# One 512-column operand in the feed-forward up products, and operands laid at one byte modulo 512

## The chip, the cores and the metric

The kernel runs on one core of one Trainium2 chip. The metric is the device time of one execution in microseconds (us). Each version is timed in several runs, and one further execution is recorded by the profiler; all rows of the profile come from that one.

## The reference

Three transformer-like blocks run one after the other on one sequence of 256 tokens with 1024 channels, in float32. Block 1 is two kinds of attention with a merge, and a product-key expert layer (PEER). Block 2 has two layers, each with a feed-forward, a mixer (a convolution module, then a gated recurrence called HGRN) and a second feed-forward. Block 3 has two layers of sliding-window attention with a short convolution and an MLP, with 16 extra "meta" tokens. The part that the change touches most is the feed-forward of Block 2, which is computed four times:

```python
def swiglu_ffn(x, w_in, w_out):
    gate, up = jnp.split(x @ w_in, 2, axis=-1)
    return (jax.nn.silu(gate) * up) @ w_out
```

Here w_in is 1024 by 5632 and w_out is 2816 by 1024, so the hidden width is 2816 = 22 x 128. All matrices are read once, about 476 MB in all.

## The kernel before, in words

The kernel keeps float32 accuracy with products of a reduced float format. Every operand is split into a high part (a rounded copy) and a low part (what the rounding left), and each product is made of three matmuls: high by high, high by low, low by high. `mm3` (L115 to L119) issues the three, each with its own load of the stationary operand.

Weights are streamed. `stream` (L89) loads 128 rows of 2048 floats (1 MB) by a DMA on the SP queue into one of three `raw` buffers (`load`, L104), and splits it in two halves: ScalarE (ACT) casts raw to `wh` (L99), VectorE (DVE) subtracts to get `wl` (L101). The pairs wh and wl rotate through slots (three in Block 1 and PEER, a fourth from Block 2 on, `more`). The normalised tokens stand transposed in the tile `xx`, 128 partitions by [high or low][8 channel blocks][272 tokens]; `xh` and `xl` are its two halves. A row of 272 tokens is 1088 bytes, and 256 of the 272 columns are tokens of the sequence, the last 16 the meta tokens.

There are two forms of product. In the first the weights are stationary and the tokens stream: `linear_stat` (L243) takes one half chunk of 128 output channels and runs over the 8 channel blocks, three matmuls of 256 columns each, so 24 matmuls into one half of a PSUM bank. `pair` does that twice, gate and up, so one chunk fills one PSUM bank of the tag "acc", of which there are four. In the second form the tokens are stationary and the weights stream in 512 columns: `cols_steps`, `linear_rows` (L316, L317, L319) and, in PEER and Block 3, the same loop written out (L1036, L1037, L1039; L1664, L1665, L1667).

The feed-forward (`Block2.ffn`) has 22 chunks of w_in. The first three go through `lead`, where tokens are stationary; the other 19 go through `pair`, with the transposes of the lead's hidden tiles put between the two halves (`turn`). For each chunk ACT applies silu to the gate (L1129), DVE multiplies by the up half (L1131), and `split` writes the hidden rows `hh` (ACT, L112) and `hl` (DVE, L113). Then `linear_rows` runs over 11 chunks of w_out with hh and hl stationary, into four accumulators that take all four "acc" banks.

The order of instructions on each engine is set by a planner that builds the program from the order in which the Python code issues, by its own estimates of time; engines then run their queues in order. `issue_after` pins a few instructions behind others. Tiles lie in pools that are stacked one after another in each partition's memory, each tile rounded up to 32 bytes; so the address of a tile is the sum of the pools and tiles before it.

Of the kernel before, what the change touches and what calls it, by code (L numbers as in the profile page):

```python
# [19 lines left out]
S = 256  # L20
# [6 lines left out]
class Core:  # L27
# [7 lines left out]
    def __init__(self, tc, ctx, a):  # L35
        self.tc, self.nc, self.a = tc, tc.nc, a
        nc = self.nc
        self.dram = ctx.enter_context(tc.tile_pool(name="dram", bufs=1, space=bass.MemoryType.DRAM))
        self.const = ctx.enter_context(tc.tile_pool(name="const", bufs=1))
        self.flip = 0  # L40
        self.last = self.done = self.later = None
        self.sm = ctx.enter_context(tc.tile_pool(name="sm", bufs=4))
        self.ps = ctx.enter_context(tc.tile_pool(name="ps", bufs=1, space=PSUM))
        self.ident = self.const.tile([128, 128], F32, name="ident")
        make_identity(nc, self.ident)
        self.half = self.const.tile([128, 8], F32, name="half")
        nc.gpsimd.memset(self.half, -0.5)
        self.X = [self.const.tile([128, D], F32, name=f"X{t}") for t in range(2)]
        self.xx = self.const.tile([128, 2, 8, SM], F32R, name="xx")
        self.xh, self.xl = self.xx[:, 0], self.xx[:, 1]  # L50

    def ring(self, ctx, n):
# [209 lines left out]
    def pair(self, hl, between=lambda: None):  # L262

        ps = self.acc((128, 2, S))
        self.linear_stat(hl, 0, ps[:, 0])
        between()
        self.linear_stat(hl, 1, ps[:, 1])
        return ps[:, 0], ps[:, 1]

    def stat_pairs(self, chunk, n, lead=0, row=None):  # L270

# [231 lines left out]
class Block1:  # L503
# [4 lines left out]
    def consts(self):  # L508
# [12 lines left out]
                                compare_op=OP.is_ge, fill=NEG)  # L521
        self.cmask = pool.tile([128, 128], F32R, name="cmask")
        nc.vector.tensor_copy(self.cmask, m)
        self.nmask = pool.tile([128, 2, 15], F32, name="nmask")
        nc.gpsimd.memset(self.nmask, 0.0)
        nc.gpsimd.affine_select(self.nmask, self.nmask, pattern=[[128, 2], [-16, 15]], base=-31,
                                channel_multiplier=1, compare_op=OP.is_ge, fill=NEG)
        self.valid = pool.tile([128, 1], F32, name="valid")
        nc.gpsimd.memset(self.valid, 1.0)
        nc.gpsimd.affine_select(self.valid, self.valid, pattern=[[0, 1]], base=-31,  # L530
                                channel_multiplier=1, compare_op=OP.is_ge, fill=0.0)
# [6 lines left out]
    def tiles(self):  # L538
        p = self.pool
        self.qT = {n: p.tile([128, 8, S], F32R, tag="qT" + n, name="qT" + n) for n in "ab"}  # L540
        self.kaH = p.tile([128, 8, S], F32R, tag="kaH", name="kaH")
        self.kaL = p.tile([128, 8, S], F32R, tag="kaL", name="kaL")
        self.kT2 = [p.tile([128, 4, S], F32R, name="kT2" + x) for x in "hl"]
        for x in (self.kaL, self.kT2[1]):
            self.k.nc.gpsimd.memset(x[64:128].bitcast(F32), 0.0)
        self.va = p.tile([128, 2, 512], F32, tag="va", name="va")
        self.vs = p.tile([128, 2, 128], F32, name="vs")
        self.vw = p.tile([128, 2, 128], F32, name="vw")
        self.tT2 = p.tile([128, 4, S], F32, tag="tT2", name="tT2")
        self.gb = p.tile([128, 2, 24], F32, name="gb")  # L550
        kdp = p.tile([128, 2, 4, 2, 64], F32, tag="kdp", name="kdp")
        self.kdp = [kdp[:, t] for t in range(2)]

    def heads_T(self, src, put, t):
        k = self.k
# [239 lines left out]
    def run(self):  # L795
# [42 lines left out]
        for t in range(2):  # L838
# [8 lines left out]
            if t == 1:  # L847
                for _ in mg:
                    pass
            self.turned("b", t, y)  # L850
        self.merge()

        gn = k.row("norm2_g")
# [238 lines left out]
class Block2:  # L1092
    def __init__(self, k, wc):

        self.k = k
        nc, a = k.nc, k.a
        tl = lambda n, sh, dt=F32: wc.tile(sh, dt, name=n)
        lo = tl("lo", [128, 2, 8])
        nc.scalar.dma_start(lo, a["lb_logits"])
        mx, e, s = tl("lmx", [128, 8]), tl("le", [128, 2, 8]), tl("ls", [128, 8])  # L1100
# [16 lines left out]
    def ffn(self, l, f, gn):  # L1117
        k, nc = self.k, self.k.nc
        with ExitStack() as ctx:
# [26 lines left out]
                pass  # L1146
            for c in range(lead, 22):
                k.last = last if lead and c < lead + 2 else None
                hd = hidden(k.pair(k.stream(w[c]), lambda: later and turn(*later.pop())), S)
                k.split(hh[:, c], hl[:, c], hd)  # L1150
            g2, gn = self.gain(l, 4 * f + 1), k.row(None, src=gn)
            k.linear_rows(k.a["ffn_out"][2 * l + f], hh, hl, lambda t, acc: k.post_norm(t, acc, g2, 0.5, gn))
# [269 lines left out]
class Block3:  # L1422
# [3 lines left out]
    def __init__(self, k, wc):  # L1426
        self.k, self.wc = k, wc
        k.w2k, k.pt = 5, 2
        nc, a = k.nc, k.a
        tl = lambda n, sh, dt=F32: wc.tile(sh, dt, name=n)  # L1430
        self.XM = tl("XM", [META, D])
        nc.scalar.dma_start(self.XM, a["meta"])
        self.mx = self.meta_tile(wc, "mx", 8)
# [3 lines left out]
        self.identr = tl("identr", [128, 128], F32R)  # L1437
        nc.vector.tensor_copy(self.identr, k.ident)
        self.mask = {}
        for n, base, cm, st, w in (("causal", 0, 1, -1, 128), ("far", -1, -1, 1, 128), ("meta", 111, -1, 1, 16)):  # L1440
            m = wc.tile([128, 128], F32, tag="mask", name="mask")[:, :w]
            nc.gpsimd.memset(m, 0.0)
# [245 lines left out]
    def mix(self, l, nt):  # L1688
        k, nc, a = self.k, self.k.nc, self.k.a
        with ExitStack() as ctx:  # L1690
            k.temp(ctx, "mxt")
            pool = self.pool = ctx.enter_context(k.tc.tile_pool(name="mx", bufs=1))
            self.cw = pool.tile([128, 4, 3], F32, name="cw")
            self.cg = pool.tile([128, 4], F32, name="cg")
            nc.scalar.dma_start(self.cw, a["conv3_w"][l])
            nc.scalar.dma_start(self.cg, a["conv3_g"][l])
            self.ones = pool.tile([128, 128], F32, name="ones")
# [30 lines left out]
    def mlp(self, l, nt):  # L1728
        k, nc, a = self.k, self.k.nc, self.k.a
        with ExitStack() as ctx:  # L1730
            k.temp(ctx, "mlt")
            pool = ctx.enter_context(k.tc.tile_pool(name="ml", bufs=1))
            n0 = S + (META if nt == 3 else 0)
            hidden = {}

            def new(c):
                hidden[c] = [pool.tile([128, 2, 2, SM], F32R, tag="hT", name="hT", bufs=5),
                             self.mh[c % 4] if nt == 3 else None]
                return hidden[c]

# [198 lines left out]
```

## Time and profile before

| | us |
|---|---|
| median of 3 runs | 2859.41 |
| the runs | 2859.89, 2859.41, 2853.96 |
| profiled execution, its time | 2853.05 |
| profiled execution, its span (first to last instruction) | 2851.1 |

The time of an execution is its span and some 2 us around it. PE is TensorE, its "PEld" rows are the loads of the stationary operand, which overlap the matmuls. Matmuls overlap each other, so the duration of one is longer than the distance between the starts of two; the distance is what a matmul takes of the engine's time. In windows the number after x counts the instructions that touch the window. L12 is line 12 of the kernel.

### The profile page before, as it was taken

What the parts mean: (1) busy time and instruction counts of PE and PEld (TensorE: products, weight loads), DVE (VectorE), ACT (ScalarE), POOL (GpSimd) and SP (SyncE); (2) the same over time, 40 slices, a digit from 0 to 9 for tenths busy, and PEclk for the clock granted to TensorE, in tenths of its full rate; (3) what the DMA queues carried; (4) which work ended last, traced back from release to release, by engine and by line L of the source; (5) the groups of instructions that cost most, each with busy time, mean ns of one, the idle gap of its engine ahead of it and who ended that gap; (6) DMA issues with size and microseconds to landing.
All of it is one profiled execution on the core that took longest, in us unless ns stands there. A gap on an engine that the chain in (4) does not pass through costs nothing.

```text
span 2851.1 us, 44585 instructions
## 1 busy us (share of the span) xinstructions
PE 2744.9 (96%) x18132; PEld 2481.8 (87%) x18132; DVE 1786.7 (63%) x3018; ACT 1364.5 (48%) x2302; POOL 294.8 (10%) x314
## 2 busy tenths in 40 slices
PE   7899979999999999999999999999999999999999
PEld 6787979989999888988899899897998878889897
DVE  6757698775555556547865555676645665466654
ACT  5544445544444555444544444524444454454543
POOL 2101650000000000003300000151001110000100
PEclk9989999999999999999999999999999999999999
DMA  5423436896565555554255455524554334433452
GB/s 207 152 97 134 150 121 254 288 321 219 204 215 205 192 192 198 201 190 167 87 188 190 165 209 189 196 89 148 193 192 142 134 116 156 161 133 121 161 192 104
DMA packets 105982, 496.74 MB, mean 174 GB/s; under 512 B 11040, under 2 KB 44320, under 8 KB 50224
## 3 DMA queue, kind: packets, MB, share of 16 engines
q1 hardware_dynamic: 61632, 443.15, 44.8%
q10 hardware_dynamic: 44144, 50.74, 5.4%
q8 instruction: 142, 2.33, 0.3%
q14 instruction: 64, 0.52, 0.1%
HBM read 476.03 MB, written 17.83 MB: 173 GB/s over the span
## 4 chain that ended last, share of the span: by engine, by line
PE 63%; issue 23%; DVE 7%; POOL 3%; ACT 3%; DMA 1%; POOLq 0%; ACTq 0%; DVEq 0%
PE acc L119 6%; PE acc L117 6%; PE acc L118 6%; PE tp L119 4%; PE tp L117 4%; PE tp L118 4%; PE o L1037 4%; PE o L1036 4%; PE o L1039 4%; PE o L316 2%; PE o L317 2%; PE o L319 2%; DVE wl L101 1%; PE o L1667 1%; PE o L1664 1%
## 5 line engine op out<-in xcount | busy, mean ns | idle before, releaser
L101 DVE TENSOR_TENSOR wl<-raw,wh 128x1024 fp32r<-128x1024 f32 x808 | 972.0, 1224 | 633.9 <-ACT wh L99 633.2
L99 ACT CAST wh<-raw 128x1024 fp32r<-128x1024 f32 x848 | 862.4, 1041 | 712.2 <-PE acc L118 234.9
L118 PE MATMUL acc<-xx,wh 128*128 128x256 f32 x1504 | 423.9, 282 | 0.0
L119 PE MATMUL acc<-xx,wl 128*128 128x256 f32 x1504 | 423.4, 281 | 0.0
L117 PE MATMUL acc<-xx,wh 128*128 128x256 f32 x1504 | 423.2, 281 | 0.0
L117 PE MATMUL tp<-xx,wh 128*128 128x256 f32 (+1 forms) x1440 | 410.7, 285 | 5.6 <-ACT ga L1020 5.6
L119 PE MATMUL tp<-xx,wl 128*128 128x256 f32 (+1 forms) x1440 | 409.0, 284 | 2.1 <-DVE wl L101 2.1
L118 PE MATMUL tp<-xx,wh 128*128 128x256 f32 (+1 forms) x1440 | 408.6, 284 | 0.0
L117 PEld LDWEIGHTS acc<-xx,wh 128*128 128x128 f32 x1504 | 284.9, 189 | 0.3 <-ACT xs L278 0.3
L119 PEld LDWEIGHTS acc<-xx,wl 128*128 128x128 f32 x1504 | 285.1, 190 | 0.0
L118 PEld LDWEIGHTS acc<-xx,wh 128*128 128x128 f32 x1504 | 283.0, 188 | 0.0
L117 PEld LDWEIGHTS tp<-xx,wh 128*128 128x128 f32 x1440 | 274.0, 190 | 9.1 <-ACT ga L1020 6.0
L118 PEld LDWEIGHTS tp<-xx,wh 128*128 128x128 f32 x1440 | 274.1, 190 | 2.5
L119 PEld LDWEIGHTS tp<-xx,wl 128*128 128x128 f32 x1440 | 273.5, 190 | 2.5 <-DVE wl L101 2.5
L117 PE MATMUL acc<-wh,xx 128*128 128x256 f32 (+2 forms) x672 | 228.3, 341 | 2.5 <-ACT xx L112 2.2
L118 PE MATMUL acc<-wl,xx 128*128 128x256 f32 (+2 forms) x672 | 223.5, 333 | 5.3 <-DVE wl L101 5.3
L147 POOL TENSOR_SCALAR va<-ss 128x1 f32<-128x1 f32 (+1 forms) x49 | 24.3, 496 | 1949.8 <-ACT junk L143 1768.1
L119 PE MATMUL acc<-wh,xx 128*128 128x256 f32 (+2 forms) x672 | 221.9, 333 | 2.1 <-DVE xx L113 2.1
L1037 PE MATMUL o<-wl,wth 128*128 128x512 f32 x512 | 200.2, 391 | 2.1 <-DVE wl L101 2.1
L1036 PE MATMUL o<-wh,wth 128*128 128x512 f32 x512 | 200.7, 392 | 0.0
L1039 PE MATMUL o<-wh,wtl 128*128 128x512 f32 x512 | 159.6, 390 | 0.0
L118 PEld LDWEIGHTS acc<-wl,xx 128*128 128x128 f32 x672 | 132.2, 197 | 16.7 <-DVE wl L101 6.9
(508 smaller groups left out, 4853.4 us busy)
## 6 DMA issues: line engine op xcount, KB each, us to landing
raw<-in_ffn_in_dram SPq DMA_DIRECT2D x88, 1024.0 KB, 4.9
raw<-in_peer_u_dram SPq DMA_DIRECT2D x64, 1024.0 KB, 5.0
raw<-in_peer_v_dram SPq DMA_DIRECT2D x64, 1024.0 KB, 4.9
raw<-in_ffn_out_dram SPq DMA_DIRECT2D x44, 1024.0 KB, 4.9
raw<-in_w_up_dram SPq DMA_DIRECT2D x32, 1024.0 KB, 4.9
raw<-in_w_down_dram SPq DMA_DIRECT2D x32, 1024.0 KB, 4.9
gd<-gt ACTq DMA_DIRECT2D x16, 1024.0 KB, 5.9
G<-gd ACTq DMA_DIRECT2D x16, 1024.0 KB, 7.0
```

Of the source, the lines that this page charges most:

```text
L99: nc.scalar.copy(h[:, c], r[:, c])
L101: eng.tensor_tensor(l[:, c], r[:, c], h[:, c].bitcast(F32), op=OP.subtract)
L117: mm(out, ah, bh, start=start, stop=False)
L118: mm(out, ah, bl, start=False, stop=False)
L119: mm(out, al, bh, start=False, stop=stop)
L316: mm(acc[t][h], hi[:, k, ts], wv[0][:, h], start=st, stop=False)
L317: mm(acc[t][h], hi[:, k, ts], wv[1][:, h], start=False, stop=False)
L319: mm(acc[t][h], lo[:, k, ts], wv[0][:, h], start=False, stop=sp)
L1036: mm(acc[t][h], wh, vh[:, h], start=st, stop=False)
L1037: mm(acc[t][h], wh, vl[:, h], start=False, stop=False)
L1039: mm(acc[t][h], wl, vh[:, h], start=False, stop=sp)
L1664: mm(acc[t][h], xh, wh[:, h], start=st, stop=False)
```

## The change

The up products of the feed-forward get a function of their own. In each of the 8 steps of a half chunk the high weights are loaded once and multiply a 512-column operand, the high and the low tokens side by side (two runs of 256 columns, 8704 bytes apart), into both halves of a PSUM bank; the low weights then multiply the high tokens into the first half. The halves are added afterwards: ACT copies the second half out, DVE adds the first.

The other part is where tiles lie. X and xx move from the pool at the start into a pool after the small tiles; tiles that nothing uses (`pad`) and a reordering move the operands of the matmuls to the same byte modulo 512 as the weights; hT in the MLP gets rows of 384 in place of 272 tokens; and xx is seen with rows of 256 tokens (1024 bytes) until the merge of Block 1, and with rows of 272 (1088 bytes) from there on.

```diff
-        self.X = [self.const.tile([128, D], F32, name=f"X{t}") for t in range(2)]
-        self.xx = self.const.tile([128, 2, 8, SM], F32R, name="xx")
+
+        self.sm.tile([128, 23], F32, name="pad", bufs=1)
+        big = ctx.enter_context(tc.tile_pool(name="big", bufs=1))
+        self.X = [big.tile([128, D], F32, name=f"X{t}") for t in range(2)]
+        self.flat = big.tile([128, 2 * 8 * SM], F32R, name="xx")
+        self.tokens(S)
+
+    def tokens(self, n):
+
+        self.xx = self.flat[:, :2 * 8 * n].rearrange("p (i k n) -> p i k n", i=2, k=8)
         self.xh, self.xl = self.xx[:, 0], self.xx[:, 1]
...
+    def wide_pair(self, hl, between=lambda: None):
+
+
+        out = []
+        for i in range(2):
+            h, l = (x.rearrange("p (e k m) -> p e k m", e=2, k=8)[:, i] for x in hl)
+            ps = self.acc((128, 2, S))
+            for kb in range(8):
+                if kb == 7:
+                    self.nc.tensor.matmul(ps[:, 0], l[:, kb], self.xh[:, kb, :S], start=False, stop=False)
+                self.nc.tensor.matmul(ps, h[:, kb], self.xx[:, :, kb, :S], start=kb == 0, stop=kb == 7)
+                if kb < 7:
+                    self.nc.tensor.matmul(ps[:, 0], l[:, kb], self.xh[:, kb, :S], start=False, stop=False)
+            if i == 0:
+                between()
+            out.append(ps)
+        return out
...
-        self.nmask = pool.tile([128, 2, 15], F32, name="nmask")
+        rows = pool.tile([128, 32], F32, name="nmask")
+        self.nmask = rows[:, :30].rearrange("p (t n) -> p t n", t=2)
...
-        self.valid = pool.tile([128, 1], F32, name="valid")
+        self.valid = rows[:, 30:31]
...
-        self.gb = p.tile([128, 2, 24], F32, name="gb")
         kdp = p.tile([128, 2, 4, 2, 64], F32, tag="kdp", name="kdp")
         self.kdp = [kdp[:, t] for t in range(2)]
+        self.gb = p.tile([128, 2, 24], F32, name="gb")
...
+        k.tokens(SM)
         self.merge()
...
+        tl("pad", [128, 48])
         lo = tl("lo", [128, 2, 8])
...
-                hd = hidden(k.pair(k.stream(w[c]), lambda: later and turn(*later.pop())), S)
+                x = []
+                for ps in k.wide_pair(k.stream(w[c]), lambda: later and turn(*later.pop())):
+                    u = k.tmp.tile([128, S], F32, tag="u", name="u", bufs=4)
+                    nc.scalar.copy(u, ps[:, 1])
+                    nc.vector.tensor_tensor(u, ps[:, 0], u, op=OP.add)
+                    x.append(u)
+                hd = hidden(x, S)
...
+        tl("pad0", [128, 16])
         self.XM = tl("XM", [META, D])
...
+        tl("pad1", [128, 16])
         for n, base, cm, st, w in (("causal", 0, 1, -1, 128), ("far", -1, -1, 1, 128), ("meta", 111, -1, 1, 16)):
...
+            pool.tile([128, 8], F32, name="pad")
             nc.scalar.dma_start(self.cw, a["conv3_w"][l])
...
+            pool.tile([128, 64], F32, name="pad")
             n0 = S + (META if nt == 3 else 0)
...
-                hidden[c] = [pool.tile([128, 2, 2, SM], F32R, tag="hT", name="hT", bufs=5),
+                hidden[c] = [pool.tile([128, 2, 2, 384], F32R, tag="hT", name="hT", bufs=5)[:, :, :, :SM],
```

## Rows read from the trace of the kernel before

**Rows 1.** The page: span, busy time by engine, the chain that ended last.
```profile
span 2851.1 us, 44585 instructions
PE 2744.9 (96%) x18132; PEld 2481.8 (87%) x18132; DVE 1786.7 (63%) x3018; ACT 1364.5 (48%) x2302; POOL 294.8 (10%) x314
...
PE 63%; issue 23%; DVE 7%; POOL 3%; ACT 3%; DMA 1%; POOLq 0%; ACTq 0%; DVEq 0%
```
**Rows 2.** Windows: feed-forward up products, feed-forward down products, PEER's down products.
```profile
core 0: us, PE busy (x) PEld busy (x) DVE busy (x) ACT busy (x) POOL busy (x), PEclk, DMA share, GB/s
...
2012.00:2112.00 100.00, 100.00 (x847) 100.00 (x846) 54.45 (x72) 47.55 (x72) 0.00 (x0) 1.00 0.55 186
1248.00:1294.00 46.00, 46.00 (x199) 36.87 (x198) 20.64 (x20) 16.86 (x18) 0.00 (x0) 1.00 0.54 187
...
1063.00:1100.00 37.00, 37.00 (x165) 30.65 (x164) 20.77 (x28) 19.52 (x28) 0.00 (x0) 1.00 0.58 200
```
**Rows 3.** Timeline of PE (start us, duration us), up products, twelve starts apart.
```profile
2079.47 0.28 PE L117 MATMUL acc<-xx,wh 128*128 128x256 f32 x1
...
2080.89 0.28 PE L117 MATMUL acc<-xx,wh 128*128 128x256 f32 x1
```
**Rows 4.** Timeline of PE: feed-forward down, twelve starts apart; PEER down, 24 apart.
```profile
2124.75 0.39 PE L316 MATMUL o<-wh,hh 128*128 128x512 f32 x1
...
2127.55 0.39 PE L316 MATMUL o<-wh,hh 128*128 128x512 f32 x1
...
1055.19 0.39 PE L1036 MATMUL o<-wh,wth 128*128 128x512 f32 x1
...
1060.63 0.39 PE L1036 MATMUL o<-wh,wth 128*128 128x512 f32 x1
```
**Rows 5.** Timeline of PE: MLP down and HGRN's i and g, each twelve starts apart.
```profile
2828.91 0.39 PE L1664 MATMUL o<-wh,hT 128*128 128x512 f32 x1
...
2831.66 0.39 PE L1664 MATMUL o<-wh,hT 128*128 128x512 f32 x1
...
1935.88 0.40 PE L117 MATMUL acc<-wh,xx 128*128 128x512 f32 x1
...
1938.66 0.40 PE L117 MATMUL acc<-wh,xx 128*128 128x512 f32 x1
```
**Rows 6.** Groups by line, 2012 to 2112 us: busy us, mean ns, idle before and releaser.
```profile
L119 PEld LDWEIGHTS acc<-xx,wl 128*128 128x128 f32 x282 | 53.4, 189 | 0.0
...
L101 DVE TENSOR_TENSOR wl<-raw,wh 128x1024 fp32r<-128x1024 f32 x36 | 44.0, 1222 | 47.9 <-ACT wh L99 47.9
L99 ACT CAST wh<-raw 128x1024 fp32r<-128x1024 f32 x36 | 37.6, 1045 | 46.6 <-PE acc L118 46.6
L113 DVE TENSOR_TENSOR hl<-hd,hh 128x256 fp32r<-128x256 f32 x18 | 7.6, 420 | 0.0
L1131 DVE TENSOR_TENSOR hd<-acc,s 128x256 f32<-128x256 f32 x18 | 7.5, 419 | 0.0
L112 ACT CAST hh<-hd 128x256 fp32r<-128x256 f32 x18 | 7.3, 408 | 7.3 <-DVE hd L1131 7.3
L1129 ACT ACTIVATE s<-acc 128x256 f32<-128x256 f32 x18 | 6.8, 377 | 0.0
```
**Rows 7.** Waits of ACT and DVE, 2012 to 2112 us: total us, times, longest us.
```profile
ACT wh L99 <- PE acc L118: 46.6, 18, 2.6
ACT hh L112 <- DVE hd L1131: 7.3, 18, 0.4
...
DVE wl L101 <- ACT wh L99: 47.9, 18, 2.8
```
**Rows 8.** Products with a stationary tile of 30 columns: group of loads, and PE's timeline.
```profile
L117 PEld LDWEIGHTS acc<-wh,Xs 128*30 128x30 f32 x32 | 3.9, 123 | 3.5 <-ACT Xs L112 2.9
...
129.68 0.28 PE L117 MATMUL acc<-wh,Xs 128*30 128x256 f32 x1
...
130.73 0.28 PE L117 MATMUL acc<-wh,Xs 128*30 128x256 f32 x1
```

## The prediction, made before the change was run

> **What bounds the kernel now.** I read the page first: TensorE (PE) is busy for 96% of the span, and 63% of the chain that ended last is PE itself [rows 1]. So what a PE product costs counts almost everywhere, and the other engines count where they hold PE up. Then the windows by stage [rows 2]: in the up products of a feed-forward layer (2012 to 2112 us) and in its down products (1248 to 1294) PE is busy for the whole window at a granted clock of 1.00, which is the 2.4 GHz level. VectorE (DVE) is busy for 54.45 of 100 us there, ScalarE (ACT) for 47.55, and the DMA share is 0.55. These stages are bound by how fast PE takes products, and by nothing that lands or is computed beside it.
>
> The "us" of one product is no price, since products overlap (0.28 us each, but one starts every 0.12 us). The price is the distance between starts, read from the timeline by two rows that are a counted number of products apart:
> - 256 columns, up products: from 2079.47 to 2080.89 are 12 products, so 1.42 / 12 = 118.3 ns [rows 3].
> - 512 columns, down products of the feed-forward: 12 products from 2124.75 to 2127.55, 2.80 / 12 = 233.3 ns [rows 4].
> - 512 columns, down products of PEER (L1036 to L1039): 24 products from 1055.19 to 1060.63, 5.44 / 24 = 226.7 ns [rows 4].
> - 512 columns, down products of Block 3's MLP: 2.75 / 12 = 229.2 ns; 512 columns in hgrn's i and g projection, where rows of xx are the stationary side: 2.78 / 12 = 231.7 ns [rows 5].
>
> The second and third are the telling pair. Both load a stationary tile of 128 columns and stream 512 columns, in the same order of six, with PE never idle, yet they differ by 6.6 ns. The code has one difference between them that fits. In PEER every tile between the weights' slots and wth/wtl is a multiple of 512 bytes (58 of 1024, two of 8192), so both operands of a product begin at one byte modulo 512. In the feed-forward, the wk pool holds two rows of 8 floats (64 bytes) and wc2 holds 256 bytes, so hh and hl lie 320 bytes off modulo 512. In the MLP and with xx, the rows are 272 floats = 1088 bytes long, so each step shifts by 64 bytes and the products run through all shifts; their mean (229.2, 231.7) lies between the two. I take this as the cause; no run shows it apart yet.
>
> **The change part by part.**
>
> *The wide product.* Chunks 3 to 21 of each feed-forward go through wide_pair: 19 x 4 = 76 chunks, each 2 x 8 = 16 steps, 1216 steps. A step was three products of 256 columns, 3 x 118.3 = 355.0 ns. It becomes one of 512 (h on xh and xl together) and one of 256 (l on xh). The same 768 columns stream; one stationary load in three goes, with what a product costs beyond its columns. By rows 3 and 4, (226.7 - 118.3) / 256 = 0.423 ns per column, which leaves 118.3 - 108.4 = 9.9 ns for each product when the bytes agree. For the 256-column product I keep 118.3: it is the old L119 in the same role. For the 512-column one the trace has no row with xx on the streaming side; the rows of xx stay 1088 bytes apart in Block 2, so the bytes agree at one step in eight, and the nearest rows are the two mixed ones, 229.2 and 231.7. I take 230.5. A step then costs 348.8, saving 6.2 ns, and 1216 x 6.2 = 7.5 us. The ends are 226.7 (12.2 us) and 236.6, twice a 256-column product (nothing). A gain beyond the first is small: with a load of only 30 columns, which takes 123 ns in place of 189, the 256-column products come every 1.05 / 9 = 116.7 ns [rows 6, 8], so a lighter load is worth at most 1.6 ns, 2 us in all.
>
> A figure from the Trainium skill speaks against a large gain here: "TensorE: Matmul & The Clock Gate", section Back-to-back issue gap, has N / 2.4 + 2.5 ns for an isolated product at full clock. By it a step would fall from 327.5 to 325.0, 3.0 us in all, and operand bytes would not enter. The trace has 118.3 where it gives 109.2, and two prices for 512 columns where it gives one, 215.8.
>
> *What the wide product adds.* Its sum stands in two halves of a PSUM bank, so each half chunk needs an ACT copy (128x256) and a DVE add (128x256): two each per chunk, 152 each in all. Nearest rows: ACT silu and cast 377 and 408 ns, DVE product 419 ns [rows 6]. Per chunk DVE has 2 x 1.222 + 0.420 + 0.419 = 3.28 us and gets 4.12; ACT has 2 x 1.045 + 0.408 + 0.377 = 2.88 and gets 3.64. PE takes 16 x 0.349 = 5.58 per chunk (5.68 before). Both fit under PE with 1.5 us to spare, so I cost them at nothing. What covers them: the casts wait 2.6 us per chunk for PE to give a slot back, and DVE then waits for the casts [rows 7], with four slots in rotation, so the split weights are some three chunks ahead. Behind the new copy on ACT stand the casts of a later chunk, behind the add on DVE their subtractions; PE waits for those only when the three chunks are used up. If the cover were gone, 0.8 us of DVE per chunk would cost up to 61 us; the third rival prices the likely part.
>
> *PSUM.* A chunk held one of the four "acc" banks and now holds two. A bank is free after the copy and add, and is wanted again two chunks later, 5 us or more after its last product: no cost. At the turn to the down products the four accumulators want all four banks; the last needs the second half of chunk 21 about 2.7 us (12 products) after PE finished it. Copy and add take 0.8 us, plus at worst a cast (1.05) and a subtraction (1.22) already ahead of them: 3.1. So 0 to 0.4 us, four times; before, silu and product (0.8 us) stood in the same place without holding PE up. Taken as 0.
>
> *One byte modulo 512, feed-forward down.* With the pads, weights, xx and hh/hl all begin at the same byte. The 22 row blocks by 2 token tiles by 2 halves by 3 products by 4 layers are 1056 products (352 each on L316, L317, L319), at 233.3 - 226.7 = 6.6 ns: 7.0 us. Ends: nothing, and 7.0.
>
> *MLP down.* hT's rows become 384 floats = 1536 bytes, so every product agrees: 768 products (L1664, L1665, L1667, 256 each) x (229.2 - 226.7 = 2.5) = 1.9 us. Ends: nothing, and 5.0 x 768 = 3.8 if rows like 231.7 are the truer mean.
>
> *Block 1.* Rows of 256 floats until the merge make xx agree there: 9 column groups x 48 = 432 products of 512 columns and the merge's 96, by 231.7 - 226.7 = 5.0 ns at most 2.6 us. PE is often idle in Block 1, so a quicker product is partly lost in the next wait: half, 1.3 us. Ends: nothing, and 2.6.
>
> *The rest* (X and xx in another pool, nmask and valid in one tile, gb behind kdp, identr and masks, a new view of xx) issues no instruction more; the 256- and 272-column up products elsewhere meet the same mix of shifts as before: nothing. No wait is added and no DMA moves.
>
> Sum: 7.5 + 7.0 + 1.9 + 1.3 = 17.7 us. The profiled execution took 2853.05 us, 1.95 more than its span, and becomes 2835.4. The median of the runs shown is 2859.41, 6.4 above the profiled one, with one of the three near the latter; taken from the median the forecast is 2841.7, and I say 2841.
>
> **The rivals.**
> *The byte does nothing.* The 6.6 ns between PEER and the feed-forward come from something else in the stages, or the unused pads don't shift the tiles as the sizes say. Then the wide product costs 233.3, saves 3.3 ns a step, 4.1 us, and nothing else moves: 2855. For it: no row shows the byte alone. Against: prices between the two exactly where the shifts are mixed [rows 5]. The skill's gap would give nearly this, 3.0 us.
> *The wide product gives nothing.* The streamed operand jumps 8704 bytes in the middle; if the jump costs what a product's start costs, a step stays at 355.0. The byte's parts remain, 10.2 us: 2849.
> *The evacuation holds PE up (slower).* If the planner puts copy, add, silu, product, cast and subtraction of a chunk in line behind both casts, DVE's round is: first cast 1.05, two subtractions 2.44, two adds 0.84, silu 0.38, product 0.42, cast 0.41, subtraction 0.42 = 5.96 us. It decides as soon as that round exceeds PE's 5.58: PE then lacks the low parts of the weights for 0.38 us per chunk, 76 x 0.38 = 29 us, less the 17.7: 2870. For it: the casts wait for PE at the head of ACT's queue [rows 7]. Against: today's chain (silu, product, cast, subtraction) interleaves with the casts at a wait of 0.4 us per chunk [rows 7].
>
> **How the numbers follow.** The forecast has 0.70; the byte does nothing 0.12; the wide product gives nothing 0.10; slower 0.08. The forecast's own ends: from the profiled level, 12.2 + 2 + 7.0 + 3.8 + 2.6 = 27.6 us off gives 2826; from the median, half of the sum gives 2851. The range reaches to the two flat rivals: 2826 to 2856. What can be told from no change is 0.2%, 5.7 us. Faster takes the forecast, the second rival and a little of the first: 0.82; same takes most of the first: 0.10; slower 0.08.
>
> **What would show it.** After: 1216 fewer PE products (16916); L316 to L316 in the feed-forward's down stage 1.36 us per six in place of 1.40; MLP down the same 1.36; a wide step 0.349 us (0.355 refutes the gain, 0.337 shows a bigger one); PE busy all through a feed-forward window, DVE near 74% and ACT near 65% of it. Waits of PE for DVE wl, or for the new add, would be the third rival. The forecast is wrong if the down stage keeps 233 ns.

## The result and the profile after

The changed kernel takes 2840.64 us (median of 6 runs, 2834.60 to 2844.57), the kernel before 2857.96 (6 runs, 2853.96 to 2859.89): a ratio of 0.9943, with a 95% interval of 0.9929 to 0.9956. That is faster by 17.3 us; the forecast was a sum of 17.7 us and a time of 2841. The profiled execution took 2840.85 us, 12.2 less than the profiled one before. That the two profiled executions are nearer to each other than the medians is taken up below.

Page of the changed kernel: the span, the busy time by engine, the chain that ended last, and the two groups of the new step.

```profile
span 2838.9 us, 42369 instructions
...
PE 2726.2 (96%) x16916; PEld 2423.5 (85%) x16916; DVE 1851.3 (65%) x3170; ACT 1417.2 (50%) x2454; POOL 295.1 (10%) x314
...
PE 61%; issue 23%; DVE 8%; POOL 3%; ACT 3%; DMA 2%; ACTq 0%; POOLq 0%; DVEq 0%
...
L288 PE MATMUL acc<-xx,wh 128*128 128x512 f32 x1216 | 414.0, 393 | 0.0
...
L290 PE MATMUL acc<-xx,wl 128*128 128x256 f32 x1064 | 298.1, 280 | 0.0
```

PE has 1216 products less, DVE and ACT 152 instructions more each, and PE is still 96% busy: the bound has not moved [rows 1]. The remaining 152 of the 1216 narrow products are the last steps of the half chunks, on L287.

Windows of the changed kernel: feed-forward up, feed-forward down, PEER's down. Columns as in [rows 2].

```profile
2000.00:2100.00 100.00, 100.00 (x576) 87.92 (x575) 69.26 (x109) 60.19 (x108) 0.00 (x0) 1.00 0.56 198
...
1250.00:1294.00 44.00, 44.00 (x196) 36.45 (x195) 19.93 (x18) 17.05 (x18) 0.00 (x0) 1.00 0.55 196
...
1063.00:1100.00 37.00, 37.00 (x165) 30.66 (x164) 20.77 (x28) 19.05 (x27) 0.00 (x0) 1.00 0.57 196
```

In the up stage PE is busy all the time at a granted clock of 1.00 as before, and takes 576 products in 100 us, where it took 847 that were smaller on average. The loads, which filled the window before (100.00), now fill 87.92. DVE went from 54.45 to 69.26, ACT from 47.55 to 60.19. PEER's down stage, which the change does not touch, has the same 165 products in its window as in [rows 2].

Timeline of PE in the changed kernel (start us, duration us): the first narrow product of L287 in two half chunks 35 apart; L342 in the feed-forward's down stage, 120 products apart; L1701 in the MLP's down stage, six products apart.

```profile
2002.64 0.28 PE L287 MATMUL acc<-xx,wl 128*128 128x256 f32 x1
...
2100.18 0.28 PE L287 MATMUL acc<-xx,wl 128*128 128x256 f32 x1
...
2114.23 0.39 PE L342 MATMUL o<-wh,hh 128*128 128x512 f32 x1
...
2141.43 0.39 PE L342 MATMUL o<-wh,hh 128*128 128x512 f32 x1
...
2816.88 0.39 PE L1701 MATMUL o<-wh,hT 128*128 128x512 f32 x1
...
2818.24 0.39 PE L1701 MATMUL o<-wh,hT 128*128 128x512 f32 x1
```

- Wide step: 97.54 us / 35 half chunks / 8 steps = 348.4 ns, where the three products took 3 x 118.3 = 355.0 [rows 3].
- Feed-forward down: 27.20 / 120 = 226.7 ns, where it was 233.3 [rows 4]: now PEER's price.
- MLP down: 1.36 / 6 = 226.7 ns, where it was 229.2 [rows 5].

Groups of the changed kernel in the window 2004 to 2102 us (busy us, mean ns | idle before it and what ended the idle time).

```profile
L109 DVE TENSOR_TENSOR wl<-raw,wh 128x1024 fp32r<-128x1024 f32 x36 | 42.5, 1222 | 1.2
L107 ACT CAST wh<-raw 128x1024 fp32r<-128x1024 f32 x36 | 36.0, 1054 | 0.0
L1182 DVE TENSOR_TENSOR u<-acc,u 128x256 f32<-128x256 f32 x36 | 15.2, 422 | 29.0 <-ACT u L1181 29.0
L1181 ACT COPY u<-acc 128x256 f32<-128x256 f32 x35 | 13.1, 374 | 17.6 <-PE acc L288 17.6
...
L1158 ACT ACTIVATE s<-u 128x256 f32<-128x256 f32 x17 | 7.1, 417 | 20.3 <-DVE u L1182 20.3
```

Waits of the changed kernel, 2000 to 2100 us (total us, times, longest).

```profile
DVE u L1182 <- ACT u L1181: 29.0, 18, 1.9
ACT s L1158 <- DVE u L1182: 21.2, 18, 1.3
ACT u L1181 <- PE acc L288: 18.8, 36, 1.0
```

The slack of [rows 7] is still there, but it has moved. Before, the casts waited for PE to give a slot back. Now ACT waits at the new copy for PE's product, DVE at the new add for the copy, and the silu for the add. PE itself waits for nothing from 2004 to 2160 us; it has no row at all in the waits of that stretch, the turn to the down products included.

The time of each stage, in us, from PE's first product of the stage to that of the next, one profiled execution of each kernel; a stage of down products ends at the start of its last product. Two short stages that were the same in all (20.7 and 7.3 us) are left out. "again" and "third" are two further profiled executions of the changed kernel, from later runs; "bytes" and "wide" are the first two experiments below.

| stage | before | after | again | third | bytes | wide |
|---|---|---|---|---|---|---|
| start to PEER's down | 562.4 | 560.8 | 561.4 | 563.5 | 557.5 | 557.4 |
| PEER's down | 554.5 | 557.0 | 557.2 | 553.6 | 557.9 | 551.7 |
| to the first feed-forward up | 21.1 | 24.4 | 21.7 | 21.4 | 20.3 | 23.5 |
| feed-forward up, each of 4 | 108.1 | 106.1 | 106.1 | 106.1 | 108.1 | 106.3 |
| feed-forward down, each of 4 | 62.2 | 60.6 | 60.6 | 60.6 | 60.6 | 62.2 |
| convolution between | 148.3 | 148.9 | 149.8 | 149.0 | 150.8 | 151.1 |
| HGRN between | 187.5 | 185.6 | 187.4 | 185.8 | 188.0 | 185.7 |
| Block 3 up to the first MLP down | 175.5 | 177.5 | 178.3 | 177.4 | 179.9 | 181.8 |
| first MLP down to the mixer | 193.7 | 193.0 | 193.9 | 193.0 | 194.0 | 193.7 |
| second mixer | 142.1 | 141.7 | 143.1 | 140.6 | 143.2 | 144.6 |
| second MLP | 156.7 | 155.5 | 155.5 | 155.5 | 155.5 | 156.7 |

Two kinds of stage stand here. The feed-forward stages, where PE never waits, repeat to 0.1 us from one execution to the next. The stages where PE waits for other engines (PEER, the mixers, Block 1) move by up to 3.6 us between the three executions of the changed kernel. The first stage, which the changed kernel shares instruction for instruction with most kernels below, ran from 556.6 to 563.5 us in them. The gains are read from the first kind: 4 x 2.0 us up and 4 x 1.7 us down. The second kind is why the difference of two single executions (12.2 us) says less than that of the medians (17.3).

### The profile page after: what moved, and what is told of

It is laid out like the page before. It is cut to its first block, busy times and chain, and to the rows that moved or that the text cites. A ratio compares the mean times of both kernels' runs of the same rounds, so it can differ in the third digit from the quotient of the medians.

```text
span 2838.9 us, 42369 instructions
## 1 busy us (share of the span) xinstructions
PE 2726.2 (96%) x16916; PEld 2423.5 (85%) x16916; DVE 1851.3 (65%) x3170; ACT 1417.2 (50%) x2454; POOL 295.1 (10%) x314
## 4 chain that ended last, share of the span: by engine, by line
PE 61%; issue 23%; DVE 8%; POOL 3%; ACT 3%; DMA 2%; ACTq 0%; POOLq 0%; DVEq 0%
PE acc L288 5%; PE tp L127 4%; PE tp L126 4%; PE tp L125 4%; PE o L1065 4%; PE o L1064 4%; PE o L1067 4%; PE acc L125 4%; PE acc L127 4%; PE acc L126 3%; PE acc L290 2%; PE o L342 2%; PE o L343 2%; PE o L345 2%; DVE wl L109 2%
## 5 line engine op out<-in xcount | busy, mean ns | idle before, releaser
L288 PE MATMUL acc<-xx,wh 128*128 128x512 f32 x1216 | 414.0, 393 | 0.0
L290 PE MATMUL acc<-xx,wl 128*128 128x256 f32 x1064 | 298.1, 280 | 0.0
L288 PEld LDWEIGHTS acc<-xx,wh 128*128 128x128 f32 x1216 | 218.7, 188 | 39.3
L290 PEld LDWEIGHTS acc<-xx,wl 128*128 128x128 f32 x1064 | 200.1, 188 | 5.6
L1182 DVE TENSOR_TENSOR u<-acc,u 128x256 f32<-128x256 f32 x152 | 64.1, 422 | 122.3 <-ACT u L1181 122.3
L127 PEld LDWEIGHTS acc<-wh,xx 128*128 128x128 f32 x672 | 129.3, 193 | 15.8 <-DVE xx L121 5.3
```

The costliest lines, as they stand in the source:

```text
L127: mm(out, al, bh, start=False, stop=stop)
L288: self.nc.tensor.matmul(ps, h[:, kb], self.xx[:, :, kb, :S], start=kb == 0, stop=kb == 7)
L290: self.nc.tensor.matmul(ps[:, 0], l[:, kb], self.xh[:, kb, :S], start=False, stop=False)
L1182: nc.vector.tensor_tensor(u, ps[:, 0], u, op=OP.add)
```

## The experiments

Two theories stood at the start. Mine: the price of a 512-column product hangs on how the bytes of its two operands lie to each other; the wide product saves what a third stationary load costs; the evacuation is free. The rivals: the byte does nothing; the wide product gives nothing; the evacuation eats the gain.

**One part alone: the bytes.** The changed kernel with the feed-forward's old `pair`:

```diff
-                x = []
-                for ps in k.wide_pair(k.stream(w[c]), lambda: later and turn(*later.pop())):
...
-                hd = hidden(x, S)
+                hd = hidden(k.pair(k.stream(w[c]), lambda: later and turn(*later.pop())), S)
```

> The changed kernel with the old pair in place of the wide product: only the places of the tiles change. My theory (what a 512-column product costs depends on whether its two operands begin at one byte modulo 512): feed-forward down products 1.36 us per six in place of 1.40, MLP down near 227.5 ns, Block 1 a little less; 7.0 + 1.9 + 1.3 = 10 us under the kernel before, so a ratio of 0.9965. First rival (the byte does nothing): the down stage stays at 1.40 per six and the time is that of the kernel before, 1.000. Up products stay at 118.3 ns per 256 columns in both.

Measured: 2851.38 us (12 runs) against 2854.41 (23 runs), ratio 0.9979 (0.9964 to 0.9993). PE's timeline in the down stage, 120 products apart:

```profile
1256.08 0.39 PE L342 MATMUL o<-wh,hh 128*128 128x512 f32 x1
...
1283.28 0.39 PE L342 MATMUL o<-wh,hh 128*128 128x512 f32 x1
```

27.20 / 120 = 226.7 ns, with the up stage at 108.1 us as before. The layout alone makes the down products cheaper, with the same PE instructions in the same order. "The byte does nothing" falls.

**One part alone: the wide product.** The kernel before, with the new function and its evacuation, and the old layout:

```diff
-                hd = hidden(k.pair(k.stream(w[c]), lambda: later and turn(*later.pop())), S)
+                x = []
+                for ps in k.wide_pair(k.stream(w[c]), lambda: later and turn(*later.pop())):
...
+                hd = hidden(x, S)
```

> The kernel before with the wide product alone, every tile where it was. My theory: a step of the up products 0.349 us in place of 0.355, 7.5 us less in all, ratio 0.9974; the down stage stays at 1.40 us per six. Rival (the wide product gives nothing, the gain is all from the bytes): step 0.355, ratio 1.000. Third rival (the added copy and add hold PE up): PE waits in the up stage and a ratio over 1.000.

Measured: 2848.94 us (12 runs) against 2854.41, ratio 0.9985 (0.9972 to 0.9998). Timeline, two half chunks 35 apart:

```profile
2003.95 0.28 PE L279 MATMUL acc<-xx,wl 128*128 128x256 f32 x1
...
2101.72 0.28 PE L279 MATMUL acc<-xx,wl 128*128 128x256 f32 x1
```

The same kernel's down products, 120 apart:

```profile
1255.73 0.39 PE L334 MATMUL o<-wh,hh 128*128 128x512 f32 x1
...
1283.73 0.39 PE L334 MATMUL o<-wh,hh 128*128 128x512 f32 x1
```

97.77 / 280 = 349.2 ns a step, and 28.00 / 120 = 233.3 ns down, unchanged. "The wide product gives nothing" falls, and each part shows in its own feed-forward stage and not in the other's. The up stage took 106.3 us here and 106.1 in the changed kernel, where a step costs 348.4 ns: once the product is wide, the layout is worth another 0.8 ns a step, 1.0 us in all. Which saving the wide product lives on is not taken apart: a step has one load less and one product less, and no run has the one without the other.

By the times of whole executions the parts do not add up well. The medians give 3.0 us for the bytes and 5.5 for the wide product, the ratios 6.0 and 4.3 us, against 20.0 and 19.4 for both together on the same chip (next run). The two parts reach what both give (15.4 to 23.4 us) only near the upper ends of their own intervals at once (10.3 and 8.0 us). In the feed-forward stages they do add up: 6.8 and 6.9 us alone, with the 1.0 us above 14.7 together. The gap has to lie in stages where PE waits: Block 3 up to its first MLP down took 175.5 us before, 179.9 and 181.8 with one part (one execution each) and 177.4 to 178.3 with both. Why is open.

**The changed kernel again**, on the same chip as those two:

> The changed kernel itself once more, on the chip of the three others, so that they can be compared with it. Ratio to the kernel before 0.994, between 0.9929 and 0.9956. The stretch from the first of PEER's down products to the start of the first wide products was 5.8 us longer in its profile than in that of the kernel before (581.4 to 575.6); if that is a matter of the execution it will not stand again, if it is the change's own it will.

Measured: 2834.46 us (6 runs), ratio 0.9932 (0.9918 to 0.9946). A later repeat on another chip:

> The changed kernel once more beside these two: ratio to the kernel before 0.993 to 0.995.

Measured: 2836.46 us (6 runs) against 2854.79, ratio 0.9940 (0.9926 to 0.9954). Both agree with the first result. The 5.8 us that PEER and the stage behind it had lost in the first profile (2.5 + 3.3) did not stay whole: the two together took 581.4 us there, 578.9 in the second execution and 575.0 in the third, against 575.6 in the one profile of the kernel before.

**Equal bytes for the streamed operand too.** If the same byte is the best case on either side, then the wide product should want it as well. The changed kernel with 1024-byte rows of xx up to the last feed-forward's up products:

```diff
-        k.tokens(SM)
         self.merge()
...
+            if l == f == 1:
+                k.tokens(SM)
```

> The changed kernel with the rows of xx 1024 bytes apart not only until Block 1's merge but until the last down products of Block 2, so that the bytes agree at every step of the wide product. My theory: the 512-column product falls from the mixed 230.6 to 226.7 ns, 1216 x 3.9 = 4.7 us; the 288 products of the output projections of Blocks 1 and 2 and the 192 of HGRN's i and g fall by some 4.5 ns, 2.2 us; together 7 us under the changed kernel, 2834, ratio to before 0.992. Rival (equal bytes help only where the token side is loaded, not where it streams): the wide step stays at 348.5 ns and only 2 us come off. A second rival: 256-column products get dearer with equal bytes, some 5000 of them by 1 ns, and 5 us are given back.

Measured: 2842.17 us (6 runs), ratio 0.9950 (0.9934 to 0.9967), no better than the changed kernel. Two half chunks 35 apart:

```profile
2011.45 0.28 PE L287 MATMUL acc<-xx,wl 128*128 128x256 f32 x1
...
2110.15 0.28 PE L287 MATMUL acc<-xx,wl 128*128 128x256 f32 x1
```

98.70 / 280 = 352.5 ns a step against 348.4. So the expectation missed in sign: equal bytes at every step are dearer than rows that run through all distances. The starts in the trace show which product it is: over 70 half chunks the 512-column product went from 230.6 to 235.2 ns and the 256-column one from 117.7 to 117.3, so the second rival falls. HGRN's i and g products, where the same rows of xx are loaded and the weights stream, did get cheaper, twelve products apart:

```profile
1938.14 0.39 PE L125 MATMUL acc<-wh,xx 128*128 128x512 f32 x1
...
1940.86 0.39 PE L125 MATMUL acc<-wh,xx 128*128 128x512 f32 x1
```

2.72 / 12 = 226.7 ns, where it was 231.7 [rows 5]. What holds when the weights stream and the token side is loaded does not hold when xx streams: that is the first rival. One thing more changes with the rows of 1024 bytes: the two runs of the wide operand lie 8192 in place of 8704 bytes apart, and no run separates that from the distance.

**Which distance, stationary side.** An unused tile ahead of hh shifts hh and hl against the weights, by another amount in each of the four layers:

```diff
+            pool.tile([128, (16, 32, 48, 64)[2 * l + f]], F32, name="shift", bufs=1)
```

> The changed kernel with an unused tile ahead of hh, of another size in each of the four feed-forwards: hh and hl lie 64, 128, 192 and 256 bytes past the weights' byte modulo 512. Nothing else differs between the four down stages, which took 60.6 us each with the bytes equal and 62.2 us in the kernel before (320 bytes past). My theory (the byte sets the price): the four lengths differ, each between 60.5 and 62.3 us, and none is shorter than 60.5. Rival (the 1.6 us came from something else that the change moved): all four stay at 60.6. The up stages stay at 106.1.

The second kernel has (80, 96, 112, 8) in place of (16, 32, 48, 64):

> The same with 320, 384, 448 and 32 bytes. My theory: 62.2 us in the first feed-forward, which then has the distance of the kernel before; the second and third between 60.5 and 62.3; 32 bytes tells whether the steps are as fine as that. Rival: all four stay at 60.6.

Measured (one execution each: 2846.32 and 2844.72 us), per product of the down stage over 120 products:

| bytes between | 0 | 32 | 64 | 128 | 192 | 256 | 320 | 384 | 448 |
|---|---|---|---|---|---|---|---|---|---|
| ns | 226.7 | 233.3 | 233.3 | 232.4 | 228.9 | 226.7 | 233.3 | 232.4 | 228.9 |

The 0 is the changed kernel's. Rows of the first kernel, for 64, 192 and 256 bytes, each pair 120 products apart:

```profile
1254.52 0.39 PE L342 MATMUL o<-wh,hh 128*128 128x512 f32 x1
...
1282.52 0.39 PE L342 MATMUL o<-wh,hh 128*128 128x512 f32 x1
...
1761.62 0.39 PE L342 MATMUL o<-wh,hh 128*128 128x512 f32 x1
...
1789.08 0.39 PE L342 MATMUL o<-wh,hh 128*128 128x512 f32 x1
...
2115.93 0.39 PE L342 MATMUL o<-wh,hh 128*128 128x512 f32 x1
...
2143.13 0.39 PE L342 MATMUL o<-wh,hh 128*128 128x512 f32 x1
```

28.00, 27.46 and 27.20 us. The price is a function of the distance, and it repeats after 256 bytes, not 512. The kernel before stood at 320 bytes, which is among the dearest places.

**Which distance, streamed side.** Rows of 1024 bytes as above, begun 64, 128, 192 and 256 bytes past the weights' byte in the four layers:

```diff
-    def tokens(self, n):
+    def tokens(self, n, at=0):
-        self.xx = self.flat[:, :2 * 8 * n].rearrange("p (i k n) -> p i k n", i=2, k=8)
+        self.xx = self.flat[:, at:at + 2 * 8 * n].rearrange("p (i k n) -> p i k n", i=2, k=8)
...
+        k.tokens(S, 16)
...
+            if l == f == 1:
+                k.tokens(SM)
+            else:
+                k.tokens(S, [32, 48, 64][2 * l + f])
```

> As the kernel with rows of 1024 bytes, whose up stages took 107.4 us with equal bytes (106.1 in the changed kernel, whose rows step through all distances), but the rows of xx begin 64, 128, 192 and 256 bytes past the weights' byte in the four feed-forwards. Theory now: the price of a wide step goes by this distance alone. The changed kernel's own steps then give 344.5 ns at 64, 349.7 at 128, 345.1 at 192 and 348.3 at 256 bytes, and 304 steps of a stage 104.9, 106.4, 105.1 and 106.1 us. Rival (the price depends also on the steps that went before, as equal bytes cost 357 ns among mixed steps and 352 in a row): the four lengths don't follow this order.

The second kernel takes 320, 384, 448 and 32 bytes:

> The same with 320, 384, 448 and 32 bytes. Theory: 346.2 ns a step at 320 and 348.1 at 384 bytes, so 105.4 and 106.0 us for the first two stages; 448 bytes stands only at the last, reordered step of the changed kernel and 32 bytes nowhere, so these two are open, between 104.9 and 108.2 us. Rival: another order, or all near 107.4 as with equal bytes in a row.

Measured (one execution each: 2841.42 and 2844.72 us), ns per step; the 0 is the kernel with 1024-byte rows above, "mixed" the changed kernel:

| bytes between | 0 | 32 | 64 | 128 | 192 | 256 | 320 | 384 | 448 | mixed |
|---|---|---|---|---|---|---|---|---|---|---|
| ns | 352.5 | 349.2 | 350.4 | 351.7 | 352.5 | 352.5 | 350.4 | 351.6 | 352.5 | 348.4 |

Timeline of the first kernel at 64 bytes, half chunks 35 apart:

```profile
1142.77 0.28 PE L287 MATMUL acc<-xx,wl 128*128 128x256 f32 x1
...
1240.89 0.28 PE L287 MATMUL acc<-xx,wl 128*128 128x256 f32 x1
```

The second at 32 bytes, half chunks 35 apart:

```profile
2006.96 0.28 PE L287 MATMUL acc<-xx,wl 128*128 128x256 f32 x1
...
2104.73 0.28 PE L287 MATMUL acc<-xx,wl 128*128 128x256 f32 x1
```

98.12 / 280 = 350.4 and 97.77 / 280 = 349.2. The period of 256 bytes is there again (64 and 320, 128 and 384, 192 and 448). But the expectation, that a step's price goes by its own distance and can be read off the changed kernel's mixed steps (344.5 at 64 bytes, 345.1 at 192), missed: held fixed, the same distances cost 350.4 and 352.5. The next table shows why it could not hold: mean ns of each of the eight steps of a half chunk, over 70 half chunks of the second and third feed-forward (from all starts in the trace).

| step | 0 | 1 | 2 | 3 | 4 | 5 | 6 | 7 |
|---|---|---|---|---|---|---|---|---|
| changed kernel, distance 64 x step | 357.5 | 344.2 | 350.0 | 345.0 | 348.3 | 345.8 | 348.3 | 347.6 |
| equal bytes, distance 0 at every step | 349.5 | 345.6 | 355.5 | 355.4 | 349.5 | 355.1 | 355.4 | 354.0 |

In the second row the distance modulo 512 is the same at each step, and still the steps run from 345.6 to 355.5. These means hide a sharper pattern. Starts of four wide products in a row, steps 1 to 4 of one half chunk with equal bytes:

```profile
2051.63 0.39 PE L288 MATMUL acc<-xx,wh 128*128 128x512 f32 x1
...
2051.97 0.40 PE L288 MATMUL acc<-xx,wh 128*128 128x512 f32 x1
...
2052.32 0.40 PE L288 MATMUL acc<-xx,wh 128*128 128x512 f32 x1
...
2052.69 0.40 PE L288 MATMUL acc<-xx,wh 128*128 128x512 f32 x1
```

Steps 1, 2 and 3 take 0.34, 0.35 and 0.37 us. By the unrounded starts in the trace, such a half chunk has 350, 361, 349, 350, 361 ns at its steps 2 to 6, and the half chunks before and behind it have the same cycle of three one step earlier. So one and the same step takes 361 ns in one half chunk and 350 in the next, at the same distance. The distance modulo 512 alone does not set a step's price. A cycle of three suggests that something is carried over from the steps before, but the two kinds of half chunk also read other weight addresses, and no run here takes this apart.

**Is the evacuation free?** The changed kernel with the copy and the add done twice per half chunk:

```diff
                     nc.scalar.copy(u, ps[:, 1])
+                    nc.scalar.copy(u, ps[:, 1])
+                    v = k.tmp.tile([128, S], F32, tag="v", name="v", bufs=4)
+                    nc.vector.tensor_tensor(v, ps[:, 0], u, op=OP.add)
                     nc.vector.tensor_tensor(u, ps[:, 0], u, op=OP.add)
```

> The changed kernel with a second ACT copy and a second DVE add for each half chunk of the feed-forward up products, 152 more of each, with results that nothing needs. My theory (they lie under PE): per chunk DVE goes from 4.12 to 4.96 us and ACT from 3.64 to 4.40, both under PE's 5.58, and the four up stages stay at 106.1 us. Rival (evacuation holds PE up as soon as there is more of it): the stages get longer, by up to 19 x 0.8 = 15 us each.

Measured (one execution: 2843.57 us): the four up stages take 106.1 us each, as in the changed kernel. Window of an up stage:

```profile
2000.00:2100.00 100.00, 100.00 (x577) 87.91 (x576) 80.86 (x142) 69.47 (x144) 0.00 (x0) 1.00 0.54 194
```

DVE rises from 69.26 to 80.86 and ACT from 60.19 to 69.47 of 100 us, and PE takes 577 products as against 576. Twice the evacuation costs the up stages nothing, so once does too; the down stages behind them took 0.1 us more each (60.65 in place of 60.55). The third rival falls for this stage, with as much room again.

**The wide product elsewhere.** If a step is worth 6 ns wherever PE is the bound, it should pay in PEER's up products, where they run beside the down stage, and in the second MLP. The function `wide` is `wide_pair`'s inner loop, `joined` its evacuation:

```diff
-                ps = k.tp((128, S), tag="tq")
-                k.linear_stat(hl, i, ps)
+                if c < 24:
+                    ps = k.tp((128, S), tag="tq")
+                    k.linear_stat(hl, i, ps)
+                else:
+                    ps = k.tp((128, 2, S), tag="tq")
+                    k.wide(hl, i, ps)
+                    ps = k.joined(self.rp, ps, 3)
...
-                    k.linear_stat(*p)
+                    (k.linear_stat if nt == 3 else k.wide)(*p)
```

> The changed kernel with the wide product in two more places: PEER's up chunks from 24 on (40 chunks, 640 steps) and the up chunks 3 to 15 of the second MLP of Block 3 (208 steps). Rows of xx step by 1088 bytes there too. My theory: 354 to 348.5 ns a step, 5.5 x 848 = 4.7 us less than the changed kernel, ratio to the kernel before 0.992. Rival (in these stages DVE and ACT have the evacuation of the down stage's operands to do as well, and two banks in place of four turn over): PE waits for the bank and the time is that of the changed kernel or more.

Measured: 2849.25 us (12 runs) against 2854.79, ratio 0.9978 (0.9968 to 0.9989): some 13 us slower than the changed kernel beside it (2836.46). The second MLP takes 154.0 us in place of 155.5, as it should, and PEER's down stage 551.6. But PEER's down stage begins at 578.3 us, not at some 561. The window 530 to 570 us of this kernel, columns as in [rows 2]:

```profile
530.00:570.00 40.00, 20.62 (x136) 17.68 (x134) 23.51 (x45) 15.60 (x32) 0.00 (x0) 0.74 0.82 272
```

Its waits in that window (total us, times, longest):

```profile
PE tp L295 <- DVE u L302: 16.2, 2, 13.4
DVE u L302 <- ACT u L301: 10.8, 2, 10.3
ACT u L301 <- DMA gd<-gt: 10.6, 1, 10.6
```

PE is busy for 20.62 of 40 us here, at a mean granted clock of 0.74; in the changed kernel it is 37.91 at 0.96. The chain reads from the bottom: the new copy writes `u`, whose memory the tile `gt` had held, and a DMA still reads `gt`; the add waits for the copy, PE for the add. The third rival's outcome is there, the evacuation holding PE up, but not its mechanism: the way goes through memory and not through DVE's time.

**The same, begun later.** With `c < 32` in place of `c < 24`, the first `u` is written when that DMA has long read its tile:

> The kernel with the wide product in two more places, but in PEER from chunk 32 on in place of 24 (512 steps there, 208 in the second MLP). In that kernel the copy of PEER's first wide chunk waited 10.6 us for a DMA out of the tile gt, whose memory the copy's tile takes over, and PE waited 13.7 us behind it; from chunk 32 on that DMA is long done. My theory: the wait is gone, PEER's first down product starts at 561 to 564 us again and not at 578, and 720 steps save 5.5 ns each, 4.0 us under the changed kernel: ratio to the kernel before 0.990 to 0.993. Rival: in PEER the evacuation holds PE up in every chunk, the stretch from PEER's first to last down product is over 557 us and the time is that of the changed kernel or more.

Measured: 2833.35 us (6 runs, 2828.62 to 2839.32) against 2855.25, ratio 0.9929 (0.9909 to 0.9948). PEER's down stage begins at 556.6 and takes 552.9 us, the second MLP 154.0. PE's waits between 560 and 1120 us, all of them:

```profile
PE tp L213 <- DVE xn L173: 2.5, 1, 2.5
PE o L1079 <- DVE wl L109: 1.8, 1, 1.8
```

The wait of 13.4 us is gone: from 530 to 590 us, where PE waited 16.4 us in the kernel above, it has no wait at all here. The median is the lowest of all kernels here, but its interval overlaps that of the changed kernel. That it is better than that one is shown by the second MLP alone, 1.5 us; of the 4.0 us expected the part in PEER is not shown.

## Why the prediction was right, and where its reasons were not

- **What bounds it.** PE bound by the price of its products: right. Where PE is never idle, each nanosecond of a step came back whole, 1216 x (355.0 - 348.4) = 8.0 us, against 4 x 2.0 us by stages (forecast 7.5).
- **The wide step.** 348.8 forecast, 348.4 measured. The 512-column product came at 230.6 ns (all undisturbed distances between starts), where I took 230.5 from the mixed rows [rows 5]; the 256-column one at 117.7, where I took 118.3. That the gain is what a third load costs stays an argument, since a product's start went with the load.
- **Its better end.** The 12.2 us that stood as an end of this term, at 226.7 ns for the wide product, does not follow from equal bytes: with equal bytes at every step a step cost 352.5 ns. "The bytes agree at one step in eight" is no reason for its price either. The mean of mixed rows was the right row to take, and the reason that I gave for it was not, so that it came within 0.1 ns is luck.
- **The feed-forward's down products.** 233.3 to 226.7 ns, 7.0 us forecast, 4 x 1.7 = 6.8 by stages. Cause shown: the layout alone does it, and other distances give other prices. "Modulo 512" is too strict: the period is 256 bytes, so that 320 bytes off counts as 64.
- **The MLP's down products.** 1.36 us per six forecast and measured; 1.9 us forecast, 0.7 + 1.2 = 1.9 by stages, though only the second repeats in all three profiles (the first gave 193.0, 193.9, 193.0 after 193.7).
- **Block 1.** 1.3 us forecast. Its products did get cheaper: the 512-column ones of the first 300 us that load xx started a median of 231 and 232 ns apart in the two profiles with the old layout, and 227 to 229 in five with the new one (405 distances in each). What that is worth in time is not shown: the stretch up to PEER's down products ran from 556.6 to 563.5 us in kernels that share its layout and its instructions, and took 562.4 and 557.4 us in the two with the old one.
- **The evacuation at nothing.** Right for the up stages, as the doubled one shows. DVE and ACT were forecast near 74 and 65% of the window and came to 69 and 60. The new add took 422 ns and the copy 374, as the rows that I took for them [rows 6]; in a 100 us window before, my terms (18 chunks of 3.28 us, 59.0) gave more than the 54.45 of [rows 2] too. The sum of durations overstates what the busy count shows, and I did not check it against the window that I had.
- **PSUM at the turn.** Nothing, as forecast: no wait of PE there.
- **The rivals.** The first two each fell by one run with one part alone. The third fell here, and its outcome came true in PEER's stage by another mechanism, at a price (13.4 us) that stands in no count of DVE's time: it needed the question of whose memory the new tile takes over, which my text asked of PSUM and not of the tile `u`.
- **The Trainium skill's gap.** By the formula for an isolated product in the section on the back-to-back issue gap of the Trainium skill's "TensorE: Matmul & The Clock Gate" the up stages would have gained 3.0 us and the down stages nothing; they gained 8.0 and 6.8, so the measurement decides against it for these products.
- **The level.** The forecast stood on the median shown (2859.41), which later runs put at 2854 to 2858; this shift of 1.5 to 5 us is as large as the smaller terms. The measured difference has an interval of 12.6 to 20.3 us, so that sum and median came within 0.4 us of the result is partly luck; what the stages without waits show is 8.0 + 6.8 us, with 1.2 to 1.9 from the MLP.

## What to carry to other kernels

Take the price of a matmul from the distance between starts in a stretch where PE never idles, per shape and per role of the operands, and compare two stretches that do the same: a difference of 3% between them was a layout, with the same instructions on either side. When one term of such a comparison is carried to another role (from the loaded to the streamed operand), run it alone first; here it changed sign. And when a change brings a new tile into a pool, ask who still reads the memory that it takes over: that wait reaches PE through two engines and shows in no sum of busy times.

## What the runs showed of the hardware

- The price of a 512-column product that streams weights, with a 128-column load of the token side, hangs on the distance between its loaded and its streamed operand's address, with a period of 256 bytes: 226.7 ns at 0, 233.3 at 32 and 64, 232.4 at 128, 228.9 at 192.
- With one streamed operand of two runs of 256 columns and a 256-column product behind it, the distance alone does not set the price of a step: at one fixed distance the mean steps took 345.6 to 355.5 ns, and within a half chunk 350, 361 and 349 ns came round every three steps. Rows that shift by 64 bytes a step (348.4) beat all nine fixed distances that were run (349.2 to 352.5), which also had the two runs 512 bytes nearer to each other. The mechanism is open.
- Stages in which PE never waits repeat to 0.1 us between executions, while those with waits moved by up to 3.6 us in one kernel and by 7 us among kernels alike up to there (556.6 to 563.5): a change of 0.2% can be read from the first kind where medians of six runs can't tell it.
